# Other durations in the planning clock while the S5 tables are made

## The chip, the cores and the metric

The kernel runs on one core of a Trainium2 chip. The metric is the time of one execution on the device in microseconds (us). The core has five engines with a queue of instructions each: TensorE (PE in the rows) multiplies matrices into banks of PSUM, VectorE (DVE) and ScalarE (ACT) work element by element, GpSimd (POOL) does so more slowly, and SyncE (SP) issues the transfers (DMA).

## The reference

One step of a decoder layer on a prompt of 2048 rows of 1024 numbers and on 8 samples of 4 rows, all in float32. Cut to its core:

```python
h = rms_norm(x, attn_norm)
u, q, k, v, g, z = jnp.split(h @ w_in, [c1, c2, c3, c4, c5], axis=-1)
# S5: 32 groups of 16 channels with 64 complex states each
dt = jnp.exp(log_step)[:, None]
mag = jnp.exp(A_re * dt)
lam_r, lam_i = mag * jnp.cos(A_im * dt), mag * jnp.sin(A_im * dt)
# s_t = lam * s_{t-1} + Bb u_t;  y = Re(C s) + D u; then GELU, GLU, norm
y5, s5_re, s5_im = s5_mixer(u, ...)
# GLA: chunks of 64 rows, b = cumsum(log sigmoid(z w + b) / 16)
qe, ke = qc * jnp.exp(b), kc * jnp.exp(-b)
o = mask(qe ke^T) vc + qe S
x = x + jnp.concatenate([y5, o], axis=-1) @ w_o
a, b = jnp.split(rms_norm(x, ffn_norm) @ w_up, 2, axis=-1)
x = x + (silu(causal_dwconv3(a)) * b) @ w_down
```

The outputs are the normalised rows and the new states of S5, GLA and the convolution.

## The kernel before, in words

The prompt is cut into four windows (w0 to w3) of 512 rows; w1 carries the 32 sample rows too, 544 in all. For each window the rows of x are normalised and transposed, TensorE makes the gate inputs z, the channels u, the gates' sums, q and k, then v tile by tile with the attention (GLA), then g, and then the projection by W_o's part for the attention. After the windows come the S5 scan, GLU and W_o's other half beside the first part of the feed-forward (blocks of `up`), and then a last stage of block products for the rest of it. Every float32 matrix is split into a rounded half (`hi`, float32r) and the rest (`lo`), and a product takes three matmuls. A weight block is loaded by SP, its `hi` made on ScalarE or GpSimd and its `lo` on GpSimd or VectorE, as `make` (line 666) decides from the clocks of the engines.

The program order is fixed: the instructions stand on each engine in the order in which the Python code emits them. The code of the windows emits the matmuls of its projections, and between groups of them calls `tick` (line 395). That lets generators emit pieces of other work: the tables of S5 (`gen_tables`, line 902, run by `gen_first`, line 1585), the transposed rows of the next window (`gen_hT`, line 839, which starts when five tile slots are free), the attention's tiles, S5 and GLU. How much of it comes where is decided by a planning clock (`Clock`, line 176). Each emitted instruction adds to it an assumed duration on its engine, behind the assumed ends of its inputs (`Clock.op`, line 237; the durations stand in `Engine`, line 280). A piece is emitted when its inputs have arrived on that clock, and work of low priority only while VectorE and ScalarE are at most 9 us ahead of TensorE on it. So a number in the clock changes no instruction, but its place in the queues.

The tables of S5 are made once, on VectorE, ScalarE and TensorE: from A and the step a chain of small operations on 16 partitions (exponential, sine, reciprocal, coefficients), powers by repeated products, transposes of 16 columns, copies and scalings of the powers (tiles of 64 x 144 and 64 x 288), and eight blocks, each with 16 products, two additions, transposes on TensorE and stores of Cd, Bd and Td to DRAM. GLA needs of VectorE the running sums (scans), and the product of q and k with exponentials (made on ScalarE); these products drain the banks `mm` of PSUM. Transposes and small products use the banks `bg`. Tiles are `t_L`, `t_H` (large and half) and `pair_L` (halves). Since each instruction goes through one helper, all rows show line L290 (L292 in the changed program).

Of the kernel before, what the change touches and what calls it, by code (L numbers as in the profile page):

```python
# [175 lines left out]
class Clock:  # L176
# [5 lines left out]
    def __init__(self):  # L182
        self.eng = {"PE": 0.0, "V": 0.0, "A": 0.0, "G": 0.0, "SP": 0.0}
        self.dma = 0.0
        self.ready = {}
        self.last = {}
        self.seen = {}
        self.stored = {}
        self.banks = {}
        Clock.parts = {}  # L190
# [89 lines left out]
class Engine:  # L280
# [5 lines left out]
    def __getattr__(self, name):  # L286
        fn = getattr(self.e, name)

        def call(*args, **kw):
            r = fn(*args, **kw)  # L290
            aps = [x for x in args if _names(x)]
            aps += [v for n, v in kw.items() if _names(v) and n != "accum_out"]  # L292
            out, ins = aps[:1], aps[1:]
            n = 1
            for d in out[0].shape[1:]:
                n *= d
            psum = any(str(getattr(x, "space", "")).endswith("PSUM") for x in aps)
            names = [q for x in ins for q in _names(x)]
            outs = [q for x in out + [kw[z] for z in ("accum_out",) if z in kw] for q in _names(x)]
            if name == "dma_start":  # L300
                m = 4
                for d in ins[0].shape:
                    m *= d
                t_ = self.c.dma_op(self.k, m, *([] if self.c.span(x)[0] else q for x, q in ((out[0], outs), (ins[0], names))), out[0], ins[0])
                return r
            if self.k == "PE":
                if kw.get("is_t") or name == "transpose":
                    cost = 0.005 + 1e-3 * n
                elif str(ins[0].dtype).endswith("float32r"):
                    cost = max(n / 2400 + 0.004, 0.11)  # L310
                else:
                    cost = max(4 * n / 2400, 0.11)
            elif self.k == "A":
                cost = 0.05 + 0.87e-3 * n
                table = TABLES.get(args[2] if len(args) > 2 else kw.get("func"))
                if table not in (None, self.table):
                    self.table = table
                    cost += 1.3
            elif self.k == "G":
                cost = 0.3 + 0.165 * n if kw.get("op") == ALU.pow else 0.12 + (2.15e-3 if name == "tensor_tensor" else 0.88e-3) * n  # L320
            else:
                fast = name in ("tensor_copy", "tensor_scalar") and not psum
                cost = 0.07 + (0.52e-3 if fast else 1.04e-3) * n
            t_ = self.c.op(self.k, cost, outs, names)
            return r

        return call
# [98 lines left out]
def kernel(ctx: ExitStack, tc: tile.TileContext, ins, outs):  # L426
# [17 lines left out]
    clock = Clock()  # L444
# [3 lines left out]
    PE, V, A, G, SP = (Engine(clock, k, e) for k, e in (  # L448
        ("PE", nc.tensor), ("V", nc.vector), ("A", nc.scalar), ("G", nc.gpsimd), ("SP", nc.sync)))
# [1134 lines left out]

    def gen_first():
        yield from gen_tables()
        flags.add("tables")

    s5 = [[bg.add(4 + hf, gen_s5(hf, q)) for q in range(4)] for hf in range(2)]
# [393 lines left out]
    for w in range(NWIN):  # L1983
        bg.most = MOST[w]
        smp = w == SW
        n = XC if smp else WT
        pieces = ((0, 272), (272, 544)) if smp else ((0, 512),)
        bg.drain(hT[w, 0], hT[w, 1], *([hT["s"]] if smp else []))
        if w == 0:
            setup_masks()  # L1990
            bg.add(2, gen_first())
# [624 lines left out]
    for kind, c, j in items:  # L2616
# [13 lines left out]
        for p in (1, 2, 3, 6, 4, 7, 5):  # L2630
# [23 lines left out]
            elif end:  # L2654
# [5 lines left out]
                while late and late[0] in stage and (p not in (1, 2) or kind == "down"):  # L2660
                    q = late.pop(0)
# [49 lines left out]
```

## Time and profile before

| | before |
|---|---|
| median of three runs | 2420.09 us (2413.03 to 2422.62) |
| profiled execution | 2419.89 us, span 2418.2 us |
| mean granted clock of TensorE | 0.971 of 2.4 GHz |
| TensorE busy | 2282.5 us, 94% |
| VectorE busy | 1545.2 us, 64% |
| ScalarE busy | 896.8 us, 37% |
| GpSimd busy | 539.0 us, 22% |

The span runs from the first to the last instruction; the rest of the profiled execution lies around it. Busy shares are averages over stages with different limits. Where TensorE is 94% busy, its timeline shows the few places where it waits, and behind each wait stands what ended it. A granted clock below 1.00 in a stretch means that TensorE ran part of it at 1.2 GHz.

### The profile page before, as it was taken

What the parts mean: (1) busy time and instruction counts of PE and PEld (TensorE: products, weight loads), DVE (VectorE), ACT (ScalarE), POOL (GpSimd) and SP (SyncE); (2) the same over time, 40 slices, a digit from 0 to 9 for tenths busy, and PEclk for the clock granted to TensorE, in tenths of its full rate; (3) what the DMA queues carried; (4) which work ended last, traced back from release to release, by engine and by line L of the source; (5) the groups of instructions that cost most, each with busy time, mean ns of one, the idle gap of its engine ahead of it and who ended that gap; (6) DMA issues with size and microseconds to landing.
All of it is one profiled execution on the core that took longest, in us unless ns stands there. A gap on an engine that the chain in (4) does not pass through costs nothing.

```text
span 2418.2 us, 32048 instructions
## 1 busy us (share of the span) xinstructions
PE 2282.5 (94%) x11809; PEld 1933.0 (80%) x11809; DVE 1545.2 (64%) x2743; ACT 896.8 (37%) x1634; POOL 539.0 (22%) x645
## 2 busy tenths in 40 slices
PE   7798999999999899999998998999999998999998
PEld 5577877777787689999998997887888776777776
DVE  6777547866633467654436655666666778686887
ACT  3243144434422453243233113344443435343444
POOL 5245425546432435631010010000000000000011
PEclk9899999999999999999999999999999999999999
DMA  6124546426653723344544752222222478676754
GB/s 170 62 94 132 149 121 196 115 83 200 174 168 112 252 93 106 114 143 121 168 166 142 249 177 62 68 81 87 79 79 79 147 232 267 226 247 215 242 184 151
DMA packets 357021, 359.72 MB, mean 149 GB/s; under 512 B 56546, under 2 KB 274842, under 8 KB 356864
## 3 DMA queue, kind: packets, MB, share of 16 engines
q1 hardware_dynamic: 356512, 357.53, 47.0%
q8 instruction: 93, 1.52, 0.3%
q14 instruction: 64, 0.52, 0.1%
q10 hardware_dynamic: 352, 0.15, 0.0%
HBM read 250.99 MB, written 106.62 MB: 148 GB/s over the span
## 4 chain that ended last, share of the span: by engine, by line
PE 61%; DVE 16%; ACT 6%; issue 4%; POOL 3%; DMA 1%; SPq 0%; ACTq 0%; DVEq 0%; POOLq 0%
PE all L290 42%; DVE t_L L290 13%; PE mm L290 11%; PE bg L290 8%; ACT t_L L290 5%; DVE t_H L290 2%; DVE pair_L L290 2%; POOL t_H L290 1%; POOL t_L L290 1%; POOL pair_L L290 1%; DMA t_L<-in_w_o_dram 0%; ACT t_H L290 0%; ACT pair_L L290 0%; DMA t_L<-Wd 0%; SPq L290 0%
## 5 line engine op out<-in xcount | busy, mean ns | idle before, releaser
L290 PE MATMUL all<-t_L,t_L 128*128 128x512 f32 (+4 forms) x7358 | 1472.2, 361 | 51.0 <-DVE t_L L290 20.0
L290 PEld LDWEIGHTS all<-t_L,t_L 128*128 128x128 f32 (+2 forms) x7358 | 1280.0, 189 | 236.4 <-DVE t_L L290 36.0
L290 DVE TENSOR_TENSOR t_L<-t_L,t_L 128x1024 fp32r<-128x1024 f32 (+9 forms) x636 | 553.0, 896 | 175.5 <-ACT t_L L290 116.3
L290 ACT ACTIVATE t_L<-t_L 128x1024 fp32r<-128x1024 f32 (+8 forms) x450 | 361.9, 825 | 440.8 <-DVE t_L L290 360.3
L290 PE MATMUL mm<-t_L,t_L 128*128 128x512 f32 (+2 forms) x2160 | 491.5, 384 | 15.4 <-DVE t_L L290 12.3
L290 PEld LDWEIGHTS mm<-t_L,t_L 128*128 128x128 f32 (+1 forms) x2160 | 382.6, 191 | 100.5 <-issue 17.5
L290 POOL TENSOR_SCALAR rr<-ss 128x1 f32<-128x1 f32 (+1 forms) x51 | 19.7, 386 | 1044.7 <-ACT pair_L L290 955.2
L290 DVE TENSOR_TENSOR t_L<-t_L,all 128x512 f32<-128x512 f32 (+2 forms) x268 | 172.4, 643 | 101.8 <-PE all L290 37.9
L290 POOL TENSOR_SCALAR t_L<-t_L 128x1024 fp32r<-128x1024 f32 (+1 forms) x91 | 117.4, 1298 | 320.5 <-PE all L290 146.7
L290 POOL TENSOR_TENSOR t_L<-t_L,t_L 128x1024 fp32r<-128x1024 f32 x49 | 136.3, 2784 | 51.8 <-ACT t_L L290 39.6
L290 ACT ACTIVATE t_L<-all 128x512 f32<-128x512 f32 (+2 forms) x134 | 71.6, 539 | 191.0 <-PE all L290 186.1
L290 DVE TENSOR_TENSOR t_L<-t_L,pair_L 128x512 f32<-128x512 f32 (+2 forms) x138 | 93.4, 679 | 56.4 <-ACT pair_L L290 51.4
L290 ACT ACTIVATE pair_L<-all 128x512 f32<-128x512 f32 (+1 forms) x104 | 61.6, 593 | 154.1 <-PE all L290 134.1
L290 PE MATMUL bg<-t_L,t_L 128*128 128x256 f32 (+7 forms) x628 | 111.2, 344 | 2.3 <-DVE t_H L290 2.3
L290 DVE SCALAR_TENSOR_TENSOR t_L<-all,cw,t_L 128x351 f32<-128x351 f32 (+1 forms) x132 | 74.7, 566 | 48.0 <-ACT t_L L290 47.2
L290 PEld LDWEIGHTS bg<-t_L,t_L 128*128 128x128 f32 (+4 forms) x628 | 85.1, 183 | 24.6 <-issue 10.8
L290 ACT ACTIVATE t_L<-all,cw 128x352 f32<-128x352 f32 x66 | 42.4, 642 | 147.1 <-PE all L290 130.2
L290 ACT ACTIVATE t_L<-bg 128x512 fp32r<-128x512 f32 (+7 forms) x121 | 53.5, 461 | 103.8 <-PE bg L290 99.3
L290 DVE SCALAR_TENSOR_TENSOR t_L<-t_L,cw,t_L 128x1024 f32<-128x1024 f32 x44 | 56.5, 1285 | 24.6 <-ACT t_L L290 23.8
L290 ACT ACTIVATE junk<-bg 128x128 bf16<-128x128 f32 (+1 forms) x68 | 18.8, 276 | 120.5 <-PE bg L290 118.9
L290 ACT ACT_TABLE_LOAD x41 | 52.6, 1283 | 23.0 <-DVE t_L L290 14.7
L290 DVE TENSOR_TENSOR t_L<-pair_L,t_L 128x144 f32<-128x144 f32 (+5 forms) x107 | 54.6, 538 | 8.2 <-ACT pair_L L290 5.8
(180 smaller groups left out, 1643.4 us busy)
## 6 DMA issues: line engine op xcount, KB each, us to landing
t_L<-in_w_up_dram SPq DMA_DIRECT2D x88, 512.0 KB, 4.9
t_L<-x2d SPq DMA_DIRECT2D x80, 512.0 KB, 5.9
t_L<-in_w_in_dram SPq DMA_DIRECT2D x64, 512.0 KB, 5.5
x2d<-t_L SPq DMA_DIRECT2D x48, 512.0 KB, 3.1
gT<-t_L SPq DMA_DIRECT2D x44, 512.0 KB, 2.7
t_L<-gT SPq DMA_DIRECT2D x48, 384.0 KB, 4.8
t_L<-in_w_down_dram SPq DMA_DIRECT2D x34, 512.0 KB, 4.9
t_L<-in_w_o_dram SPq DMA_DIRECT2D x24, 512.0 KB, 5.5
```

Source lines behind the costliest of these rows:

```text
L290: r = fn(*args, **kw)
```

## The change

While the tables are made, the clock takes longer durations: 0.0135 instead of 0.004 us over the columns for a float32r matmul, 0.155 instead of 0.05 for ScalarE, 0.14 instead of 0.07 for VectorE. A VectorE instruction with two inputs or more, none in PSUM, that would start within the last two-input operation of GpSimd is taken to wait for its end. When `gen_tables` has ended, the former figures hold again.

```diff
@@ Clock.__init__
+        self.fine = True
+        self.sums = (0.0, 0.0)
@@ Engine, the durations
-                    cost = max(n / 2400 + 0.004, 0.11)
+                    cost = max(n / 2400 + (0.0135 if self.c.fine else 0.004), 0.11)
...
-                cost = 0.05 + 0.87e-3 * n
+                cost = (0.155 if self.c.fine else 0.05) + 0.87e-3 * n
...
-                cost = 0.07 + (0.52e-3 if fast else 1.04e-3) * n
+                cost = (0.14 if self.c.fine else 0.07) + (0.52e-3 if fast else 1.04e-3) * n
+                if self.c.fine and not psum and len(aps) > 2:
+
+                    g0, g1 = self.c.sums
+                    t = max([self.c.eng["V"]] + [self.c.arrive("V", q) for q in names])
+                    if g0 <= t < g1:
+                        cost += g1 - t
             t_ = self.c.op(self.k, cost, outs, names)
+            if self.k == "G" and name == "tensor_tensor":
+                self.c.sums = t_
@@ gen_first
         yield from gen_tables()
+        clock.fine = False
         flags.add("tables")
```

What it moves. First VectorE in window 0, from the reciprocal of the tables to the first products of q and k; `mm_457` and `mm_489` are the banks with q, `mm_521` and `mm_553` those with k, `t_L_319` is a table on 16 partitions. In the program before:

```order
63 L290 RECIPROCAL t_L_319<-t_L_319 16x128
64 L290 TENSOR_SCALAR t_L_319<-t_L_432 16x128
65 L290 TENSOR_TENSOR t_H_298<-t_L_319,t_H_298 16x128
66 L290 TENSOR_TENSOR t_L_319<-t_L_433,t_H_299 16x128
67 L290 TENSOR_TENSOR t_H_298<-t_H_298,t_L_319 16x128 x2
68 L290 TENSOR_TENSOR t_H_299<-t_L_433,t_H_298 16x128
69 L290 TENSOR_TENSOR t_L_319<-t_L_319,t_H_299 16x128
70 L290 TENSOR_TENSOR t_H_299<-t_H_299,t_L_319 16x128 x2
71 L290 SCALAR_TENSOR_TENSOR t_L_453<-mm_457,t_L_453 128x512
72 L290 SCALAR_TENSOR_TENSOR t_L_453<-mm_489,t_L_453 128x512
73 L290 TENSOR_TENSOR t_L_454<-mm_521,t_L_454 128x512
74 L290 TENSOR_TENSOR t_L_454<-mm_553,t_L_454 128x512
```

In the changed program, from the subtraction of the running sum (`t_L_392`) to the products of k; the banks with q are `mm_409` and `mm_441`, those with k `mm_473` and `mm_522`:

```order
46 L292 TENSOR_TENSOR t_L_392<-t_L_392,pair_L_400 128x512 x2
47 L292 SCALAR_TENSOR_TENSOR t_L_405<-mm_409,t_L_405 128x512
48 L292 SCALAR_TENSOR_TENSOR t_L_405<-mm_441,t_L_405 128x512
49 L292 TENSOR_TENSOR t_L_319<-t_H_298,sm_321 16x128
50 L292 TENSOR_TENSOR t_L_319<-t_H_299,sm_321 16x128
51 L292 TENSOR_SCALAR t_L_319<-t_L_319 16x128 x3
52 L292 SCALAR_TENSOR_TENSOR t_L_319<-t_L_319 16x128 x2
53 L292 TENSOR_SCALAR pair_L_320<-t_L_319 16x128
54 L292 TENSOR_SCALAR t_L_319<-t_L_319 16x128
55 L292 SCALAR_TENSOR_TENSOR t_L_319<-t_L_319 16x128 x7
56 L292 SCALAR_TENSOR_TENSOR t_L_319<-t_L_319,pair_L_320 16x128
57 L292 TENSOR_TENSOR t_L_406<-mm_473,t_L_406 128x512
```

The 17 operations of the table's exponential, which stood ahead of the scans, now stand between the products of q and of k; the sine, the reciprocal and the coefficients come behind all four products.

Second, VectorE in the projection W_o of window 0. Before, the end of the first block of tables stands there, from its last four products to the drains `mm` of W_o:

```order
222 L290 TENSOR_TENSOR t_L_1441<-pair_L_1242,t_L_1091 128x144
223 L290 TENSOR_TENSOR t_L_1442<-pair_L_1242,t_L_1091 128x144
224 L290 TENSOR_TENSOR pair_L_1235<-pair_L_1152,t_L_1068 128x128
225 L290 TENSOR_TENSOR pair_L_1152<-pair_L_1235,t_L_1068 128x128
226 L290 TENSOR_TENSOR t_L_1441<-t_L_1441,t_L_1442 128x576
227 L290 TENSOR_TENSOR pair_L_1235<-pair_L_1235,pair_L_1152 128x512
228 L290 TENSOR_TENSOR t_H_1391<-t_H_1391,mm_1463 128x512
```

In the changed program the copies and scalings of the powers stand between the four drains of W_o's second half there, and `bg_1488` holds the transposed sample rows:

```order
199 L292 COPY t_L_1419<-pair_L_1255 64x144 x8
200 L292 TENSOR_TENSOR t_H_1401<-t_H_1401,mm_1431 128x512
201 L292 SCALAR_TENSOR_TENSOR t_L_1379<-t_L_1379,rr_1383,gain 32x1024
202 L292 TENSOR_TENSOR pair_L_1255<-pair_L_1255,mm_1449 128x512
203 L292 COPY t_L_1463<-t_L_1419 64x288
204 L292 TENSOR_SCALAR t_L_1463<-t_L_1419 64x288 x3
205 L292 TENSOR_SCALAR t_L_1419<-t_L_1419 64x32
206 L292 COPY t_L_1419<-t_L_1419 64x32
207 L292 TENSOR_SCALAR t_L_1419<-t_L_1419 64x32
208 L292 COPY t_L_1419<-t_L_1419 64x32
209 L292 TENSOR_SCALAR t_L_1419<-t_L_1419 128x32
210 L292 TENSOR_TENSOR t_H_1447<-t_H_1447,mm_1474 128x512
```

The first block went from here to the first matmuls of window 1, behind its gate sums; the copies came here from the attention of window 0.

Third, TensorE at the end of window 1. Before, from the transposed x rows of window 2 (`t_L_3034` and the like) over those of the sample's output (`t_H_2973`) and a product with it:

```order
1448 L290 MATMUL bg_3274<-ident,t_L_3034 128x128
1449 L290 MATMUL bg_3274<-ident,t_L_3036 128x128
1450 L290 MATMUL bg_3281<-ident,t_H_2973 128x32 x4
1451 L290 MATMUL mm_3297<-t_L_2845,t_L_3286 64x512
1452 L290 MATMUL mm_3297<-t_L_2846,t_L_3286 32x512
```

In the changed program at this place, from a group of W_o (`mm_3048`) over the sample's state (`bg_3086` and the like), the transposes and the product of the last block of tables (`bg_3110`, `bg_3117`), to the sample's output (`pair_L_2402`):

```order
1424 L292 MATMUL mm_3048<-t_L_2806,t_L_2970 128x512
1425 L292 MATMUL bg_3086<-pair_L_2291,t_L_2401 64x128 x8
1426 L292 MATMUL bg_3096<-pair_L_2291,t_L_2401 64x128 x8
1427 L292 MATMUL bg_3110<-ident,pair_L_2696 128x128 x4
1428 L292 MATMUL bg_3117<-t_L_3062,t_H_1508 16x128 x4
1429 L292 MATMUL bg_3125<-pair_L_2291,t_L_2401 64x128 x8
1430 L292 MATMUL bg_3135<-pair_L_2291,t_L_2401 64x128 x8
1431 L292 MATMUL bg_3172<-ident,pair_L_2402 128x32 x4
1432 L292 MATMUL mm_3189<-t_L_2692,t_L_3177 64x512
```

Before, the last block lay far ahead of this place, and 16 of the 32 transposes of x rows ahead of the sample's output, 16 behind the product with it. Now the last block lies here, and all 32 transposes follow behind the last group of W_o and the first groups of S5.

## Rows read from the trace of the kernel before

**Rows 1.** Busy time (and count) of each engine by stretch, then TensorE's granted clock.

```profile
140.00:180.00 40.00, 35.51 (x165) 29.02 (x166) 37.40 (x52) 23.66 (x44) 24.99 (x20) 0.91 0.34 108
190.00:203.00 13.00, 4.78 (x22) 3.64 (x21) 13.00 (x19) 0.00 (x0) 9.63 (x5) 0.79 0.24 74
213.00:218.00 5.00, 5.00 (x42) 4.43 (x39) 4.89 (x19) 0.77 (x2) 0.00 (x0) 1.00 0.42 101
220.00:340.00 120.00, 120.00 (x738) 97.73 (x738) 65.56 (x185) 40.22 (x84) 44.44 (x24) 1.00 0.44 118
```

**Rows 2.** Timeline of TensorE, first wait: start, duration, operation, [wait before, releaser].

```profile
71.84 12.34 PE L290 MATMUL mm<-t_L,t_L 128*128 128x512 f32 x40 [10.71 <-DVE t_L L290]
```

**Rows 3.** Timeline of VectorE around the first wait.

```profile
52.92 2.19 DVE L290 COPY decay<-t_L 128x8 f32<-128x8 f32 x1
...
58.65 4.26 DVE L290 TENSOR_TENSOR t_L<-t_L,pair_L 128x512 f32<-128x512 f32 x2
...
63.33 0.91 DVE L290 SCALAR_TENSOR_TENSOR t_L<-t_L 16x128 f32<-16x128 f32 x3
...
71.03 1.27 DVE L290 SCALAR_TENSOR_TENSOR t_L<-mm,t_L 128x512 f32<-128x512 f32 x2
```

**Rows 4.** Timelines of GpSimd and ScalarE around the first wait.

```profile
51.91 3.18 POOL L290 TENSOR_TENSOR t_L<-t_L,t_L 128x1024 fp32r<-128x1024 f32 x1
...
59.69 2.68 POOL L290 TENSOR_TENSOR t_L<-t_L,t_L 128x1024 fp32r<-128x1024 f32 x1
70.98 7.07 POOL L290 TENSOR_TENSOR t_L<-t_L,t_L 128x1024 fp32r<-128x1024 f32 x3 [8.61 <-ACT t_L L290]
...
67.96 4.85 ACT L290 ACTIVATE t_L<-t_L 128x1024 f32<-128x1024 f32 x5
```

**Rows 5.** Timelines of VectorE and TensorE at the second wait.

```profile
146.11 5.56 DVE L290 COPY t_L<-t_H 64x144 f32<-64x144 f32 x8
...
152.02 3.10 DVE L290 TENSOR_SCALAR t_L<-t_L 64x288 f32<-64x288 f32 x4
...
157.68 2.79 PE L290 MATMUL bg<-ident,pair_L 128*128 128x128 f32 x12 [3.59 <-DVE pair_L L290]
```

**Rows 6.** Timelines of VectorE and TensorE at the third wait.

```profile
189.88 1.30 DVE L290 TENSOR_TENSOR t_L<-pair_L,t_L 128x144 f32<-128x144 f32 x2
...
202.19 0.67 DVE L290 TENSOR_TENSOR pair_L<-pair_L,pair_L 128x512 f32<-128x512 f32 x1
...
203.01 1.09 PE L290 MATMUL bg<-ident,pair_L 128*128 128x128 f32 x4 [8.23 <-DVE pair_L L290]
203.74 4.86 PE L290 MATMUL mm<-t_L,t_L 128*128 128x512 f32 x12
```

**Rows 7.** Timeline of VectorE, first and last row of the second block.

```profile
213.17 0.52 DVE L290 TENSOR_TENSOR t_L<-pair_L,t_L 128x144 f32<-128x144 f32 x2
...
217.20 0.69 DVE L290 TENSOR_TENSOR t_H<-t_H,t_H 128x512 f32<-128x512 f32 x1
```

**Rows 8.** Timelines of SP, VectorE and TensorE before window 2; DMA: KB, median us to landing.

```profile
333.99 5.02 SPq L290 DMA_DIRECT2D Td<-t_L  x8
...
350.21 2.02 SPq L290 DMA_DIRECT2D t_L<-in_x_prompt_dram  x4
...
t_L<-in_x_prompt_dram SPq DMA_DIRECT2D x4, 512.0 KB, 5.9
...
370.35 5.73 DVE L290 SCALAR_TENSOR_TENSOR t_L<-t_L,rr,gain 128x1024 f32<-128x1024 f32 x4
...
375.79 1.09 PE L290 MATMUL bg<-pair_L,t_L 32*64 32x128 f32 x16
...
384.58 0.43 PE L290 MATMUL bg<-ident,t_H 32*128 32x32 f32 x4 [1.82 <-DVE t_L L290]
386.57 3.67 PE L290 MATMUL mm<-t_L,t_L 128*64 128x512 f32 x8 [1.56 <-DVE t_L L290]
...
392.70 11.15 PE L290 MATMUL mm<-t_L,t_L 128*128 128x512 f32 x48
```

## The prediction

> **What bounds the kernel now.** I read the busy times first: TensorE works 94% of the span, so the change can win only where TensorE waits or runs at its lower clock. The busy times by stretch come next: from 220 to 340 us TensorE has no gap and the full clock, from 140 to 180 us the granted clock is 0.91, a mean over its two levels of 1.2 and 2.4 GHz [rows 1]. TensorE's own timeline then shows where it waits while the S5 tables are made, in window 0: 10.71 us before 71.84, 3.59 us before 157.68 and 8.23 us before 203.01, each released by VectorE [rows 2, 5, 6]. Last I read the timelines of VectorE and GpSimd over the same stretches, to see what VectorE did in these waits. The change moves instructions from early in the program to about the start of window 2; in the last stage TensorE's list is the same in both programs. So I add up four places.
>
> **Place 1, the drains of q and k in window 0.** TensorE has finished its groups at 61.13 (71.84 - 10.71) and needs a bank of PSUM that VectorE must drain. VectorE ends the subtraction of the running sum at 58.65 + 4.26 = 62.91, then makes 25 small table operations, with ScalarE between, and drains the first two banks only from 71.03 [rows 2, 3]. In the changed list these two drains stand right behind the subtraction. They need the exponential on ScalarE, about 0.97 us (4.85 for 5) [rows 4]: 62.91 + 0.97 + 0.64 (half of 1.27 for two drains) = 64.5, so TensorE would go on 7.3 us earlier. But only for twelve matmuls, as the third bank is drained behind 17 table operations that stood earlier before. At 0.30 us each (three in 0.91) [rows 3] these are 5.2 us, from 65.2 to 70.4, and the drain ends at 71.0. Twelve matmuls take 2.8 us at full clock (48 in 11.15) [rows 8] and, by that, 5.6 at half; with some of both TensorE waits again from about 68 to 71. The waits sum up to 3.4 + 3 = 6.4 instead of 10.7: 4.3 gained. The other bound: GpSimd now makes the rounded half of three more weight blocks here, where it stood idle from 62.4 (59.69 + 2.68) to 70.98 [rows 4]. A copy of 128x8 at 52.92 took 2.19 us, more than seven times the 0.30 of a larger operation, and ended at 55.11 with GpSimd's subtraction, 51.91 + 3.18 = 55.09 [rows 3, 4]. With three such holds of 2.1 each the gain is gone and 2 us more are lost. I take 2 gained, since a block's multiplication leaves VectorE free for part of the time; range from 4.3 gained to 2 lost.
>
> The diff lets only operations with two inputs wait for GpSimd, and that copy has one. The Trainium skill (SBUF — State Buffer, Who interferes with whom) says that copies and one-input scalar operations can take the port shared with GpSimd too, and that the second to issue is blocked for the whole instruction; the trace agrees for this copy. By that rule all 17 operations are exposed and place 1 loses the 2 us; by the diff's own rule only some are, and it gains up to 4.3.
>
> **Place 2, copies and scalings of the powers.** Before, eight copies (5.56 us) and four scalings (3.10) stand between the outputs of window 0's attention and their transposes: TensorE waits 3.59 us, and the lower clock around it costs 0.09 x 40 = 3.6 us [rows 1, 5]. In the changed list they stand in the projection W_o, where four banks lie between TensorE and VectorE. These 7.2 us go. What is late next: four groups of twelve matmuls give 11.2 us of cover; VectorE has there four drains (0.67 each, as the addition at 202.19) [rows 6], the copies, the scalings, one normalisation of 1.43 (5.73 for 4) [rows 8] and six small operations, about 1 us by the 0.30 of the small ones in place 1 and less for fewer columns: 13.8. So the last drain and the sample rows behind it come 2.6 us late, and behind them ScalarE and GpSimd still make the operands of window 1's first matmul, some 1 to 2 us; with part of that at half clock I take 4, from a range of 0 to 7.
>
> **Place 3, the first block of tables.** The 18 operations of a block took from 189.88 to 202.86 with GpSimd at work, and from 213.17 to 217.89 while it was idle (first and last rows shown) [rows 1, 6, 7]. TensorE waited 8.23, and the next twelve matmuls took 4.86 instead of 2.79, with four transposes 1.09: about 2.4 us of clock [rows 6, 8]. These 10.6 us go. In the changed list 84 matmuls of 272 columns stand between the last input of VectorE and this block's transposes, some 84 x 0.13 = 11 us (0.232 for 512 columns, so 0.12 to 0.14 here). Against that stand 4.7 us alone and 13.0 beside GpSimd, with two clears and a product ahead. I take 0 for a new wait and keep 5 as its other end.
>
> **Place 4, from the last table to window 2.** This one costs. Tables now end later in TensorE's list, and the last block stands on VectorE right behind a drain of W_o, while TensorE has only two small sample groups (1.09 us each) [rows 8] to do before its transposes: 0.67 + 4.7 - 2.2 = 3.2 us of wait. The sample's state follows on VectorE, three multiplications (1.43 by the nearest row), four additions and a subtraction (0.67), 7.6 us against 3.2 us on TensorE: 4.4 us before the sample's transposes, where the trace has 1.82, and behind them again about 1.56, as before [rows 8]. That is 9.2 against 3.4: 5.8 lost.
> Then the x rows of window 2, which SP issues behind the last eight table stores. Counted from the end of the block: state additions 7.6, stores 5.02, issues 2.02, landing 5.9, square 0.97, normalisation 1.43, in all 22.9; if the four rows share the way in and land twice as late, 28.8 [rows 4, 8]. TensorE gets there after 7.6 + 1.6 + 3.7 (eight matmuls at half clock) + 11.15 (W_o) + about 4 (sample and S5, from the same row) = 28 [rows 8]. So the 32 transposes, all behind W_o now, just find their rows, and each us of delay on SP or VectorE beyond that is one on TensorE. I take 1.5. Place 4 together: 7.3 lost, from 4 to 25.
>
> **Sum.** -2 - 7.2 + 4 - 10.6 + 7.3 = -8.5. The rest of the stages before the last keep their work, shifted against each other; I give that 0, with 5 either way. The profiled execution took 2419.89 us (span 2418.2), within 0.2 of the median of the runs, 2420.09: 2419.89 - 8.5 is about 2411.
>
> **Rivals.**
> *All of it is won.* Place 1 gains 4.3, window 1 starts without a wait and place 4 costs 5: -4.3 - 7.2 - 10.6 + 5 = -17.1, 2403. For it: the later blocks of tables in window 1 cost TensorE nothing before, from 220 to 340 us [rows 1]. Against it: place 2's 13.8 us on VectorE under 11.2 on TensorE.
> *GpSimd holds VectorE back at the new places.* The 17 operations at place 1 (2 lost), the block at the start of window 1 (5 lost), the copies and the wait behind them (7 lost): 2 + 5 + 7 - 7.2 - 10.6 + 7.3 = +3.5, 2423. For it: the slow rows of rows 3 and 6 lie beside GpSimd. It is also what the skill's rule on the port gives where copies and scalings are held as well. Against it: from 213 to 218, where the trace has its second block, GpSimd did nothing [rows 1].
> *Slower: window 2 waits for its x rows and weights.* The rows stand on SP behind stores that wait for VectorE's last addition, the weights behind the rows and the loads of S5. If the rows land 5.9 us later, the next weights another 5.9, with 2.7 for their subtraction (59.69), and 6 us of clock follow, under twice place 2's 3.6: -8.5 + 20.5 = +12, 2432, and up to 2440. It decides from the point where the rows land after W_o and S5 end. For it: all 32 transposes come in one piece, where half stood ahead of W_o. Against it: 22.9 against 28.
>
> **How the numbers follow.** The forecast has 0.36 (2406 to 2417), all won 0.29, held back 0.20, slower 0.15. A measurement of this kernel tells about 0.5%, 12 us, from no change: faster is under 2408, slower over 2432. All won is faster but for a tenth of it, and the forecast by a quarter: 0.35. Slower takes two thirds of the last case and a little of the third: 0.13. The rest, 0.52, is the same. The range runs from 2396 to 2435, which leaves out the ends of the first and the last case, about 2 in 10 with what I have not thought of.
>
> **What would show it.** Place 1: VectorE's first drain of q at about 64.5 and a second wait of some 3 us before the third bank. Place 2: no idle before the transposes of window 0's outputs, a wait of 3 to 4 us before window 1's first matmuls. Place 3: a block in 5 to 8 us without a wait on TensorE. Place 4: waits of about 3, 4 and 1.6 us, and transposes of x rows with under 2 us of idle. A stall of over 10 us before window 2's first matmul, or a first drain after 68, would prove the forecast wrong.

## The result, and the profile after

The changed kernel takes 2441.24 us (median of 4 runs, 2440.91 to 2442.94), the kernel before on the same chip 2421.36: a ratio of 1.0089, 95% interval 1.0068 to 1.0110. It is slower by about 20 us, where 8.5 less than before, about 2411, were forecast. The profiled execution has a span of 2439.7 us against 2418.2, so 21.5 us are to be found.

The table cuts the spans at TensorE's first matmul of each window (`mm<-t_L,wz`), at the first matmul of 352 columns, with which the stage behind window 3 begins, and at the start of the last product of that stage. Idle is the sum of the gaps between TensorE's rows; half is TensorE's busy time in the pieces in which the profile has the granted clock at 0.5, and costs half of itself. All in us.

| stage | length before | idle | half | length after | idle | half | difference |
|---|---|---|---|---|---|---|---|
| window 0 | 192.2 | 27.0 | 30.3 | 174.0 | 16.1 | 14.6 | -18.2 |
| window 1 | 196.8 | 4.4 | 5.5 | 226.5 | 24.7 | 23.6 | +29.7 |
| window 2 | 195.2 | 12.2 | 18.4 | 207.4 | 19.6 | 23.2 | +12.2 |
| window 3 | 242.7 | 16.9 | 9.1 | 236.9 | 12.5 | 7.2 | -5.8 |
| next stage | 640.1 | 19.9 | 17.1 | 640.9 | 20.6 | 19.9 | +0.8 |
| last stage | 931.1 | 42.2 | 16.2 | 933.9 | 42.2 | 22.6 | +2.8 |

Length less idle less half of half is the work at full clock, and it is the same in each stage within 2.5 us (window 1: 189.6 and 190.0). So no work was added or moved between stages: TensorE waits elsewhere, and runs at the lower clock where it waited. Window 0 gained about what was forecast (15.8 in the sum), though not where; windows 1 and 2 lost 41.9.

Busy times of three stretches, first of before, then of after (stretch, then length, busy time and count of TensorE, weight loads, VectorE, ScalarE, GpSimd; granted clock, DMA share, GB/s):

```profile
100.00:140.00 40.00, 37.82 (x207) 28.25 (x205) 12.20 (x45) 7.61 (x32) 6.02 (x7) 0.83 0.15 53
360.00:440.00 80.00, 76.62 (x426) 60.90 (x425) 62.39 (x89) 40.89 (x132) 46.87 (x59) 0.96 0.64 181
```
```profile
100.00:140.00 40.00, 40.00 (x212) 30.51 (x212) 19.98 (x45) 14.23 (x40) 9.63 (x10) 1.00 0.21 67
140.00:180.00 40.00, 35.77 (x192) 28.75 (x191) 38.30 (x49) 16.18 (x31) 31.10 (x21) 0.91 0.41 122
360.00:440.00 80.00, 59.45 (x289) 43.68 (x287) 36.76 (x67) 27.27 (x81) 35.97 (x45) 0.77 0.56 166
```

From 360 to 440 us every engine does less than before, so none is the bound there; they wait for each other. From 100 to 140 us the wait of 2.2 and the half clock of this stretch are gone: 2.2 + 0.17 x 40 = 9.0 us, at a place that the prediction does not have. And at place 2, from 140 to 180 us, nothing is won: busy time 35.77 for 35.51 and the same clock of 0.91 [rows 1, 5].

**Place 1** [rows 2 to 4]. After, timelines of TensorE, VectorE and GpSimd (start, duration, operation, count, [wait before, releaser]):

```profile
64.28 5.46 PE L292 MATMUL mm<-t_L,t_L 128*128 128x512 f32 x12 [3.71 <-DVE t_L L292]
76.55 5.63 PE L292 MATMUL mm<-t_L,t_L 128*128 128x512 f32 x16 [6.82 <-DVE t_L L292]
...
63.44 1.29 DVE L292 SCALAR_TENSOR_TENSOR t_L<-mm,t_L 128x512 f32<-128x512 f32 x2 [1.12 <-ACT t_L L292]
64.64 2.22 DVE L292 TENSOR_TENSOR t_L<-t_H,sm 16x128 f32<-16x128 f32 x2
66.79 3.53 DVE L292 TENSOR_SCALAR t_L<-t_L 16x128 f32<-16x128 f32 x3
70.35 2.77 DVE L292 SCALAR_TENSOR_TENSOR t_L<-t_L 16x128 f32<-16x128 f32 x2
...
66.81 2.42 POOL L292 TENSOR_TENSOR t_L<-t_L,t_L 128x1024 fp32r<-128x1024 f32 x1
69.20 1.04 POOL L292 TENSOR_SCALAR t_L<-t_L 128x1024 fp32r<-128x1024 f32 x1
70.33 2.34 POOL L292 TENSOR_TENSOR t_L<-t_L,t_L 128x1024 fp32r<-128x1024 f32 x1
```

The first drain comes at 63.44 and TensorE goes on at 64.28, as forecast (64.5). The second wait is 6.82 instead of 3: three of VectorE's rows among the 17 small operations take 1.6 to 2.6 us longer than 0.30 for each operation, beside GpSimd. Together 10.53 against 10.71.

**Place 3** [rows 6, 7]. After, VectorE, GpSimd and TensorE at the first block:

```profile
199.67 7.45 DVE L292 COPY t_H<-t_L 64x128 f32<-64x128 f32 x4
207.15 3.42 DVE L292 TENSOR_TENSOR t_L<-t_L,t_L 128x1024 fp32r<-128x1024 f32 x1
...
214.88 0.44 DVE L292 TENSOR_TENSOR t_L<-pair_L,t_L 128x144 f32<-128x144 f32 x2
...
218.85 0.67 DVE L292 TENSOR_TENSOR pair_L<-pair_L,pair_L 128x512 f32<-128x512 f32 x1
...
199.42 3.01 POOL L292 TENSOR_TENSOR t_L<-t_L,t_L 128x1024 fp32r<-128x1024 f32 x1
202.40 1.07 POOL L292 TENSOR_SCALAR t_L<-t_L 128x1024 fp32r<-128x1024 f32 x1
203.55 2.39 POOL L292 TENSOR_TENSOR t_L<-t_L,t_L 128x1024 fp32r<-128x1024 f32 x1
205.91 1.09 POOL L292 TENSOR_SCALAR t_L<-t_L 128x1024 fp32r<-128x1024 f32 x1
207.09 2.40 POOL L292 TENSOR_TENSOR t_L<-t_L,t_L 128x1024 fp32r<-128x1024 f32 x1
...
201.88 10.82 PE L292 MATMUL mm<-t_L,t_L 128*128 128x272 f32 x84
219.58 1.11 PE L292 MATMUL bg<-ident,pair_L 128*128 128x128 f32 x4 [6.88 <-DVE pair_L L292]
```

The block itself takes 4.7 us (214.88 to 219.52) and the cover 10.82, both as worked out. But VectorE comes to it late: the four copies ahead, which the prediction did not count, take 7.45 us beside GpSimd. One by one they take 2.88, 1.02, 2.48 and 1.03: each ends within 0.13 us of one of GpSimd's instructions, the one-input scalings as well as the sums. The wait of 8.23 is one of 6.88 in the next window.

**Place 4** [rows 8]. After, SP's queue, VectorE and TensorE from the last block to window 2:

```profile
380.17 5.87 SPq L292 DMA_DIRECT2D Td<-t_L  x8
386.14 1.95 SPq L292 DMA_DIRECT2D t_L<-in_x_prompt_dram  x4
388.14 0.75 SPq L292 DMA_DIRECT2D t_L<-Ud  x1
...
398.20 1.88 SPq L292 DMA_DIRECT2D t_L<-in_w_in_dram  x2
400.19 1.82 SPq L292 DMA_DIRECT2D pair_L<-in_x_prompt_dram  x1
...
407.26 1.37 DVE L292 TENSOR_TENSOR pair_L<-pair_L,mm 128x512 f32<-128x512 f32 x2 [17.24 <-DMA pair_L<-in_x_prompt_dram]
408.56 1.86 DVE L292 SCALAR_TENSOR_TENSOR t_L<-t_L,rr,gain 128x1024 f32<-128x1024 f32 x1
...
424.16 0.67 DVE L292 TENSOR_TENSOR t_H<-t_L,t_L 128x128 f32<-128x128 f32 x2 [4.37 <-POOL t_L L292]
...
371.61 1.09 PE L292 MATMUL bg<-ident,pair_L 128*128 128x128 f32 x4 [3.61 <-DVE pair_L L292]
...
380.75 0.60 PE L292 MATMUL bg<-ident,pair_L 32*128 32x32 f32 x4 [1.82 <-DVE pair_L L292]
...
410.56 0.45 PE L292 MATMUL bg<-ident,t_L 128*128 128x128 f32 x1 [6.43 <-DVE t_L L292]
412.31 3.46 PE L292 MATMUL bg<-ident,t_L 128*128 128x128 f32 x15 [1.30 <-DVE t_L L292]
417.32 3.68 PE L292 MATMUL bg<-ident,t_L 128*128 128x128 f32 x16 [1.55 <-DVE t_L L292]
...
426.23 2.34 PE L292 MATMUL mm<-t_L,wz 128*32 128x512 f32 x5 [3.79 <-DVE t_L L292]
```

Window 2's rows are asked for at 386.14 instead of 350.21. They land in time: ScalarE has squared the last of them by 395.98. Their scaling is late. It stands on VectorE behind the drains of W_o, and these wait 17.24 us for the other rows, those that W_o's result is added to. SP issues these only at 400.19, behind S5's first loads and window 2's weights. TensorE waits 6.43, 1.30 and 1.55 for the rows. The last wait, 3.79, is for the rows' last three `lo` halves, which VectorE makes from 425.50: ahead of them in its list stands a step of S5 (424.16), for which it waits 4.37 until GpSimd has made the step before. The clock is at half from 407.83 to 421.48 and from 424.89 to 431.72.

Window 2's longest wait behind this grew as well; the first row here is from before, the second from after:

```profile
496.77 0.49 PE L290 MATMUL bg<-pair_L,t_H 128*128 128x128 f32 x2 [3.23 <-DVE t_H L290]
```
```profile
513.87 0.77 PE L292 MATMUL bg<-pair_L,t_H 128*128 128x128 f32 x2 [8.38 <-DVE t_H L292]
```

### The profile page after: what moved, and what is told of

It reads as the page before. It is cut to its first block, busy times and chain, and to the rows that moved or that the text cites. A ratio compares the mean times of both kernels' runs of the same rounds, so it can differ in the third digit from the quotient of the medians.

```text
span 2439.7 us, 32035 instructions
## 1 busy us (share of the span) xinstructions
PE 2291.1 (94%) x11809; PEld 1938.4 (79%) x11809; DVE 1542.5 (63%) x2736; ACT 892.2 (37%) x1636; POOL 536.3 (22%) x647
## 4 chain that ended last, share of the span: by engine, by line
PE 45%; DVE 14%; ACT 6%; issue 4%; POOL 2%; DMA 2%; SPq 1%; DVEq 0%; POOLq 0%; ACTq 0%
PE all L292 39%; DVE t_L L292 12%; ACT t_L L292 6%; PE bg L292 3%; PE mm L292 3%; DVE t_H L292 2%; POOL t_H L292 1%; SPq L292 1%; DMA t_H<-in_x_prompt_dram 1%; POOL t_L L292 0%; ACT pair_L L292 0%; DMA t_L<-ydT 0%; DMA pair_L<-Wd 0%; DMA t_L<-in_w_in_dram 0%; ACT t_H L292 0%
## 5 line engine op out<-in xcount | busy, mean ns | idle before, releaser
L292 PEld LDWEIGHTS all<-t_L,t_L 128*128 128x128 f32 (+2 forms) x7358 | 1281.9, 189 | 242.7 <-DVE t_L L292 34.7
L292 DVE TENSOR_TENSOR t_L<-t_L,t_L 128x1024 fp32r<-128x1024 f32 (+7 forms) x639 | 554.9, 894 | 193.1 <-ACT t_L L292 142.2
L292 PE MATMUL mm<-t_L,t_L 128*128 128x512 f32 (+2 forms) x2160 | 493.6, 385 | 16.2 <-DVE t_L L292 15.3
L292 POOL TENSOR_SCALAR t_L<-t_L 128x1024 fp32r<-128x1024 f32 (+1 forms) x96 | 123.1, 1286 | 352.9 <-PE all L292 132.6
L292 DVE TENSOR_TENSOR t_L<-t_L,pair_L 128x512 f32<-128x512 f32 (+3 forms) x139 | 94.3, 681 | 75.6 <-ACT pair_L L292 54.0
L292 POOL TENSOR_TENSOR t_L<-t_L,t_L 128x1024 fp32r<-128x1024 f32 x46 | 125.7, 2732 | 22.2 <-ACT t_L L292 18.4
L292 PE MATMUL bg<-ident,t_L 128*128 128x128 f32 (+2 forms) x256 | 45.2, 313 | 24.5 <-DVE t_L L292 24.5
L292 POOL TENSOR_TENSOR t_H<-t_H,t_L 128x128 f32<-128x128 f32 (+5 forms) x90 | 46.8, 541 | 75.1 <-DVE t_H L292 34.3
```

## The experiments

All times in one table; ratio to before on the same chip, stage lengths from the profiled execution. In the texts on record "after" is the changed kernel and "before" the other.

| kernel | us | ratio [95%] | window 0 | 1 and 2 | 3 | next | last |
|---|---|---|---|---|---|---|---|
| before | 2421.36 | 1 | 192 | 392 | 243 | 640 | 931 |
| after | 2441.24 | 1.0089 [1.0068, 1.0110] | 174 | 434 | 237 | 641 | 934 |
| e1 | 2464.64 | 1.0174 [1.0155, 1.0194] | 173 | 425 | 263 | 652 | 932 |
| e2 | 2439.05 | 1.0070 [1.0055, 1.0085] | 173 | 432 | 240 | 641 | 934 |
| e3 | 2451.42 | 1.0129 [1.0111, 1.0147] | 189 | 385 | 283 | 643 | 930 |
| e4 | 2464.55 | 1.0181 [1.0164, 1.0198] | 174 | 423 | 266 | 642 | 930 |
| e5 | 2430.68 | 1.0039 [1.0027, 1.0051] | 174 | 432 | 234 | 640 | 930 |
| e6 | 2446.34 | 1.0102 [1.0075, 1.0129] | 195 | 418 | 242 | 640 | 929 |
| e7 | 2437.01 | 1.0062 [1.0041, 1.0083] | 190 | 435 | 225 | 639 | 933 |
| e8 | 2435.15 | 1.0052 [1.0033, 1.0071] | 193 | 451 | 213 | 626 | 930 |
| e9 | 2440.28 | 1.0084 [1.0066, 1.0102] | 195 | 416 | 237 | 640 | 930 |
| e10 | 2458.66 | 1.0166 [1.0136, 1.0196] | 173 | 427 | 261 | 643 | 930 |
| e11 | 2459.80 | 1.0162 [1.0145, 1.0179] | 191 | 403 | 260 | 651 | 929 |
| e12 | 2434.13 | 1.0064 [1.0041, 1.0087] | 174 | 430 | 242 | 641 | 930 |
| e13 | 2429.03 | 1.0039 [1.0022, 1.0056] | 174 | 417 | 242 | 641 | 934 |
| e14 (after) | 2436.26 | 1.0071 [1.0051, 1.0091] | 174 | 432 | 239 | 640 | 930 |
| e15 | 2420.47 | 1.0007 [0.9991, 1.0024] | 193 | 391 | 244 | 640 | 930 |
| e16 | 2427.90 | 1.0042 [1.0024, 1.0060] | 174 | 419 | 242 | 640 | 931 |

**Parts of the change alone (e1, e6, e7, e8, e11).** e1 turns the new figures off when window 1 begins; e8 has them only from there on:

```diff
+        if w == 1:
+            clock.fine = False
```


> The changed kernel, but with the former figures from the start of window 1. Theory A (the loss is made where the last block of tables meets the end of window 1: SP has the loads of S5 ahead of the residual rows of W_o, VectorE waits for those in its list, and the x rows of window 2 behind them): window 0 is as in the changed kernel, first matmul of window 1 near 195 us, the tables end earlier in TensorE's list, the 17 us wait of VectorE for residual rows goes, 2405 to 2417 us. Theory B (VectorE is too full in window 1 with all eight blocks beside GpSimd, the boundary only inherits it): little better than the changed kernel, 2430 to 2441 us.

> The former figures in window 0, the new ones from the start of window 1 to the end of the tables. Window 0 is then as in before (window 1's first matmul at 209 to 213). The tables end at 216 us of TensorE's work, nearly as in before (219). Theory C: windows 1 and 2 take 390 to 400 us as in before, time 2415 to 2425. Theory D (any new order of window 1 by the new figures loses at its end): windows 1 and 2 take 415 or more, time 2440 to 2465.

e6 keeps only the matmul's new duration, e7 only the rule for GpSimd sums, e11 all but VectorE's new duration (e11's edit; e6 and e7 put back the other former figures in the same way):

```diff
-                cost = (0.14 if self.c.fine else 0.07) + (0.52e-3 if fast else 1.04e-3) * n
+                cost = 0.07 + (0.52e-3 if fast else 1.04e-3) * n
```


> Only the new duration of a matmul is kept (while the tables are made); ScalarE's and VectorE's durations and the rule for GpSimd sums are the former ones. In this order the tables end a fifth earlier by TensorE's work than in after (183 us of work in place of 233). Theory C (how late the tables end decides the loss: their last blocks, S5's first loads and window 2's rows and weights meet at the end of window 1 when it is late, and not when it is early): windows 1 and 2 together take 385 to 400 us, and the time is 2400 to 2420. Theory D (the loss is one of the order as a whole, whichever table time): 2425 to 2450, with windows 1 and 2 at 410 or more.

> Only the rule that an operation of VectorE with two inputs in SBUF ends with the GpSimd sum beside it is kept (while the tables are made); all durations are the former ones. The tables end at 190 us of TensorE's work (after 233, before 219). Theory C: windows 1 and 2 take 385 to 400 us, time 2400 to 2420; whether the 18 us gained in window 0 come from this rule is read from window 1's first matmul, 194 if they do and 212 if not. Theory D: 2425 to 2450.

> The changed kernel with the former fixed duration of VectorE's operations (0.07 us in place of 0.14); the new durations of the matmul and of ScalarE and the rule for GpSimd sums stay. The tables then end at 215 us of TensorE's work (after 234, before 221), and window 2's rows are asked for 36 us of work before its first matmul (after 14, before 30). Theory E: windows 1 and 2 take 390 to 405 us, and if the new rule keeps window 0 short (window 1 at 194 to 200) the time is 2400 to 2418. Theory F: windows 1 and 2 take 410 or more, time 2425 to 2445.

No part alone is faster than before, and window 0 is short (173, 174) only where all the new figures stand in it. e6 and e7 end the tables early (last table store at 312 and 317 us, after 385) and still need 418 and 435 us for windows 1 and 2: it isn't the end of the tables as such, and theory C falls. In e8 window 1 begins at 213.4 as in before, and 1 and 2 take 451, partly since they do 22 us more of TensorE's work than before, mostly products of GLU, which window 3 then lacks; in e7 it is 11 us. In e11 windows 1 and 2 come nearest to before (403), but it loses 18 in window 3 and 11 behind it, with a wait of 10.08 before the first transposes there. e1, e3, e4 and e10 show a wait of the same size (9.99 to 10.22), where before has 5.65. It is none of after's loss, and its cause stays open; no theory foresaw the loss in window 3, and the times of e1, e3, e10 and e11 lie above both of their theories' ranges. e8's time, 2435.15, lies between its two ranges, though windows 1 and 2 are as in theory D.

**The last rows on another queue (e2), S5 later (e4), one block later (e3).** e2 issues the W_o rows of window 1 from ScalarE's queue once the tables are made, all else in the same order:

```diff
+            clock.alt = A.e if w == SW and "tables" in flags else None
```


> The changed kernel with the same order on every engine, but the residual rows of W_o in window 1, from the end of the tables on, are issued on ScalarE's queue instead of SP's. Theory A: VectorE's 17.2 us wait for these rows shrinks to under 5, the waits of TensorE before window 2 (6.4, 1.3, 1.6, 3.8 us) fall to under 5 together, 2425 to 2432 us. Theory B: the rows were not what held it, at most 3 us less, 2438 to 2442 us.

VectorE's wait of 17.24 is gone, the rows are transposed 6 us earlier, and TensorE waits 7.99 a little later. TensorE, VectorE, ScalarE and GpSimd in e2:

```profile
424.12 2.34 PE L293 MATMUL mm<-t_L,wz 128*32 128x512 f32 x5 [7.99 <-DVE t_L L293]
...
411.10 3.22 DVE L293 TENSOR_TENSOR t_L<-bg,t_L 128x512 fp32r<-128x512 f32 x5 [7.95 <-ACT t_L L293]
422.05 0.67 DVE L293 TENSOR_TENSOR t_H<-t_L,t_L 128x128 f32<-128x128 f32 x2 [7.74 <-POOL t_L L293]
...
410.46 2.07 ACT L293 ACTIVATE t_L<-bg 128x512 fp32r<-128x512 f32 x4
...
421.50 0.52 POOL L293 TENSOR_TENSOR t_L<-t_L,t_H 128x128 f32<-128x128 f32 x1
```

ScalarE copies S5's first products until 410.46 before it turns to the rows' halves, which holds VectorE's first five `lo` halves. The wait of 7.99 is for the last three, and these stand behind the same step of S5 as in after: VectorE waits 7.74 for GpSimd, which makes S5's steps until 422.02. So the next two lists were as full as SP's, and window 2 goes on only 2.1 us earlier than in after (424.12 for 426.23).

e4 starts S5 only in window 2; e3 is before with its last table block held until W_o's fourth step:

```diff
-        need = [("u", 2 * hf, q), ("u", 2 * hf + 1, q), "tables"] + ([("s5", 0, q), ("st", 0, "c")] if hf else [("us", q), "gs"])
+        need = [("u", 2 * hf, q), ("u", 2 * hf + 1, q), "tables", ("win", 2)] + ([("s5", 0, q), ("st", 0, "c")] if hf else [("us", q), "gs"])
```
```diff
+            while q == 7 and "hold" not in flags:
+                yield "idle"
```


> The changed kernel, but S5 may begin only when window 2 has begun, so that its loads do not stand on SP ahead of the residual rows of W_o. Theory A: the wait before window 2 falls to under 5 us, 2425 to 2434 us, unless S5 coming later costs it again in window 2. Theory B: 2438 us or more.

> The kernel before with its former figures, but the last block of tables is held back until W_o of window 1 has emitted its fourth step. Window 0 and most of window 1 are as before. Theory A: a wait of TensorE of 10 us or more appears before window 2, as in the changed kernel, 2432 to 2446 us. Theory B: within 4 us of before, 2417 to 2425 us.

e4 takes 11 less in windows 1 and 2 and 29 more in window 3. But 8 of the 11 are work of TensorE that has left these windows, so hardly anything is won. e3 takes 7 less than before in windows 1 and 2, at 14 us less work there, so 7 are lost, and 40 more in window 3, of which 17 are work. Late rows (they are loaded at 373 there) cost little in e3, in which S5 has not begun: TensorE waits 4.80 for them.

**The copies (e5, e13, e14, e15, e16).** e5 is after in its own order, with the four copies of place 3 made by ScalarE:

```diff
+        clock.cp = A.e
         for r_ in range(2):
             for q in range(2):
                 V.tensor_copy(ss5[r_ * 64 : r_ * 64 + 64, q::2], s0v[q * 64 : q * 64 + 64, r_])
+        clock.cp = None
```


> The order of after, word for word; only the four copies t_H<-t_L 64x128 of the first table block, which took 7.45 us on VectorE at 199.67 beside the GpSimd sums of window 1, are made by ScalarE at the same place in the program. Theory A (these copies, held beside the GpSimd sums, are what TensorE's wait of 6.88 at 219.58 rests on, and the wait costs the time): VectorE comes to the block some 7 us earlier, the wait falls under 1.5 us, window 1's first matmul stays at 194 and window 2's comes at 411 to 414, and the time is 2431 to 2435. Theory B (what is gained early in window 1 is given back at its end, where TensorE waits for rows and tables): the wait falls as well, window 2 begins at 418 to 421, and the time is 2438 to 2442.

ScalarE and TensorE in e5:

```profile
195.58 0.87 ACT L292 ACTIVATE t_H<-t_L 64x128 f32<-64x128 f32 x2
...
214.02 0.66 PE L292 MATMUL bg<-ident,pair_L 128*128 128x128 f32 x4 [1.48 <-DVE pair_L L292]
...
223.85 2.43 PE L292 MATMUL mm<-t_L,t_L 128*128 128x272 f32 x11 [3.14 <-ACT pair_L L292]
```

Two copies take 0.87 us there. The wait of 6.88 becomes 1.48, but 3.14 more come right behind it, and window 2 begins only 1.4 us earlier: theory B early on. The time is 10.6 under after's first result. e14, after once more on e5's chip, takes 2436.26, between the two values expected, with 10.6 us at half clock in the last stage instead of 22.6.

> The changed kernel itself once more, on the chip of e12 and e13. 2438 to 2443 if its time is as steady from chip to chip as that of before; under 2435 if e5's 2430.68 was the chip or the granted clock.

So 5.6 of the 10.6 are e5's. But the profiles do not show them at the copies: windows 0 to 2 together are as long in e5 as in e14 within 0.5 us, and 4.8 of the difference stand in window 3, at the same idle time within 1 us and with 3.3 us at half clock instead of 11.4. So what the copies cost by their wait is not shown to be 5 us. e13 against e12 gives 5.1 (on one chip), with intervals of the ratios that overlap.

> As e12, word for word, with the four copies of the first block on ScalarE as in e5. If the copies cost time by the wait behind them: 5 to 10 us under e12. If e5's gain was the granted clock of the later stages: within 3 us of e12, or to either side by what the clock's half-speed stretches differ.

e15 does the same in before, with the copies and scalings of the powers too (place 2), and e16 in e12:

> The kernel before, in its order, with the one-input operations of two table steps made by ScalarE at the same places of the program: the copies and scalings of the powers (5.56 us and the scalings behind them on VectorE, before 157.68) and the copies into the first block. If place 2 was sized rightly (the wait of 3.59 us goes, and the lower clock around it): window 1's first matmul at 205 to 208 in place of 212.4, and the time is 2413 to 2417 if the rest stays. If what is gained in window 0 is given back before window 3, as in after: window 3 begins at 602 to 606 as in before, time 2418 to 2424. Slower, if ScalarE, which goes through its list in order, comes late with the halves of the weights behind the copies: 2424 to 2430.

> e12 with both sets of copies and the scalings on ScalarE. The copies into the first block were worth 5 us (e13 against e12). The copies of the powers stand in the projection W_o of window 0 in this order, where no wait of TensorE rests on them, so they should be worth 0 to 2: 2426 to 2430. If they were what the wait of 1.46 before window 1 rests on, window 1 begins 1 to 2 us earlier.

e15 is before's time within the noise. The wait of 3.59 [rows 5] is gone from its place and others stand there, in all 5.22. TensorE in e15:

```profile
154.04 3.05 PE L293 MATMUL mm<-t_L,t_L 128*128 128x512 f32 x12 [1.94 <-ACT t_H L293]
158.27 0.63 PE L293 MATMUL bg<-ident,pair_L 128*128 128x128 f32 x4 [1.18 <-DVE pair_L L293]
159.94 0.63 PE L293 MATMUL bg<-ident,pair_L 128*128 128x128 f32 x4 [1.05 <-DVE pair_L L293]
161.62 1.09 PE L293 MATMUL bg<-ident,pair_L 128*128 128x128 f32 x4 [1.05 <-DVE pair_L L293]
```

**The rows of window 2 (e9, e10, e12).** e9 is before, with these four loads held back to W_o's third step; the tables and S5's first loads stay:

```diff
+        while w == SW + 1 and "hold" not in flags:
+            yield "idle"
         if w:
             yield from room(5)
```


> The kernel before, with one edit: the rows of window 2 (four loads t_L<-x_prompt, at 350 us in before, when the tables end) are asked for only after the second W_o step of window 1, at about 385 us as in after. The tables and S5's first loads stay where they are. Theory E (the lead of window 2's rows decides the loss at the end of window 1: rows asked for after S5's loads come behind them, and VectorE's scalings of the rows behind the W_o drains): window 2's first matmul comes 10 to 20 us later than in before, at 419 to 430, and the time is 2432 to 2445. Theory F (the rows are only one of several waits there, and when one goes or comes another moves): window 2 begins at 409 to 416, time 2418 to 2430.

The loads go out at 391.24 instead of 350.21, window 2 begins at 434.0 instead of 409.1, and the time is 2440.28, that of after (2.4 of the 24.9 stand in window 0 already). So holding these rows back, with what the planner then puts in their place, is enough to lose all of it. How, these rows of TensorE in e9 tell:

```profile
400.58 5.85 PE L290 MATMUL mm<-t_L,t_L 128*64 128x512 f32 x15 [11.06 <-DVE t_L L290]
...
410.87 11.48 PE L290 MATMUL mm<-t_L,t_L 128*128 128x512 f32 x41 [4.44 <-POOL t_L L290]
...
429.19 1.12 PE L290 MATMUL bg<-ident,t_L 128*128 128x128 f32 x4 [5.09 <-DVE t_L L290]
```

Only the last of the three is for the rows; the first is the sample's W_o step, whose input stands on VectorE behind S5 operations that took the place of the rows' scalings (one of them waits 4.00 for GpSimd). The sum is as in theory E, the waits are not.

e10 lets after's rows go when two tiles are free instead of five; e12 puts the tables first in window 1, so that they end, and the rows are loaded, earlier:

```diff
-            yield from room(5)
+            yield from room(2 if w == SW + 1 else 5)
```
```diff
+        if w == SW:
+            for e in bg.gens:
+                if e[0] == 2 and e[3].__name__ == "gen_first":
+                    e[:2] = [0, -1]
+            bg.gens.sort(key=lambda e: e[:2])
```


> The changed kernel, with one edit: the rows of window 2 wait for two free tiles in place of five, so the first two loads come 25 us of TensorE's work before after's, and the last two a little before; the tables still end late (237 us of work, 234 in after). Theory E: the wait of 6.43 us before the transposes of window 2's rows goes, window 2's first matmul comes at 405 to 412, and the time is 2420 to 2432. Theory F: window 2 begins at 415 to 425 and the time is 2435 to 2450.

> The changed kernel with one rule more: from the start of window 1 the tables come before all other work that is merged in. Window 0 is word for word that of after up to the end of the table preparation; the tables end at 214 us of TensorE's work (after 234, before 221), and window 2's rows are asked for 38 us of work before its first matmul (after 14, before 30). Theory E (the tables' late end, and with it the rows' late loads, is what costs after its gain): window 1 at 194, windows 1 and 2 take 388 to 400 us, and the time is 2400 to 2418. Theory F (the end of window 1 loses in every order but that of before): windows 1 and 2 take 410 or more, time 2425 to 2445.

e10's first rows load at 324, but the last table block then waits on VectorE for tiles that are still being stored (1.17 and 4.25), and TensorE for the block 8.70. VectorE's wait for the W_o rows is there as in after, 16.70, and behind it TensorE waits 8.17 before window 2: with the rows of window 2 transposed early it begins at 421.06, as in after (420.65). In e12 all rows go out at 345.50, no transpose of them waits, and window 2 takes 192.6, less than in before. Window 1 takes 237.4. TensorE in e12:

```profile
217.92 1.12 PE L292 MATMUL bg<-ident,pair_L 128*128 128x128 f32 x4 [7.10 <-DVE t_L L292]
...
228.83 1.12 PE L292 MATMUL bg<-ident,t_H 128*128 128x128 f32 x4 [5.56 <-DVE t_H L292]
...
402.25 3.67 PE L292 MATMUL mm<-t_L,t_L 128*64 128x512 f32 x8 [4.16 <-DVE t_L L292]
...
413.16 0.50 PE L292 MATMUL mm<-t_L,t_L 128*128 128x512 f32 x1 [3.33 <-ACT t_L L292]
```

Two waits of table blocks at its start, and at its end the sample's step again and the halves of W_o's weights, behind S5's copies on ScalarE. Theory F, then, for after: each repair tried moves the wait to the next user of the same lists. The best of these, e5, e13 and e16 (1.0039, 1.0039 and 1.0042, after 1.0071 and 1.0089), stay above before; no kernel here beats it.

## Why the prediction was wrong

By its own terms, in the profiled executions:

- *Place 1*, "2 gained": 0.2 in the waits (10.53 against 10.71). The forecast of the first drain and of a second wait was right, the second wait's size not: 6.82 for 3. The reason given for taking 2, that a multiplication on GpSimd leaves VectorE free, is not in the rows: the last of VectorE's operations at 66.79 ends at 70.32, GpSimd's scaling beside it at 70.24. The trace agrees with what the Trainium skill states of the port shared with GpSimd (SBUF — State Buffer, Who interferes with whom): one-input operations are held too, three scalings of 16x128 for 3.53 us beside a GpSimd sum of 2.42 and a scaling of 1.04, where three operations of that size took 0.91 [rows 3].
- *Place 2*, -7.2 + 4: 1.1 lost. The wait of 3.59 is gone, but shorter ones and another piece at half clock stand in the same 40 us (0.3 more busy time, 0.91 as before), and window 1's first matmul waits 1.35 instead of 4. e15 shows the same for the copies alone, with the wait gone and the granted clock still 0.91: the clock's 3.6 was no gain that hangs on this wait. It was also too large, since in part of the half clock TensorE waited; its 5.7 us of work there cost 2.9.
- *Place 3*, 10.6 gained, "I take 0 for a new wait and keep 5 as its other end": the new wait is 6.88, with 2.0 of clock (3.9 us of TensorE's work at half behind it, until 223.51), so 1.7 were gained. I counted the block and its cover, and not what VectorE has in its list ahead of the block: four one-input copies beside GpSimd.
- Not priced: 9.0 gained from 100 to 140 us, where a wait of 2.2 before `bg<-t_H,t_H` went, and the half clock with it. I took the three longest waits of window 0 and left out this fourth one, whose stretch cost 9.0 with its clock.
- *Place 4*, "Place 4 together: 7.3 lost, from 4 to 25": this is the step that failed. Windows 1 and 2 lost 41.9, less 8.9 for the first block: 33.0. The last block and the sample were sized about rightly, 5.8 forecast and 7.0 lost: the waits are shorter together than forecast (3.61, 1.82 and 0.69 for 3.2, 4.4 and 1.6), but 12.5 us of work behind them ran at half clock (from 370.28 to 387.35), where before has 5.5. The x rows failed: "I take 1.5", and they cost 19.9, 13.1 in waits (6.43 + 1.30 + 1.55 + 3.79) and 6.8 for 13.6 us of work at half clock around them. The other 6.1 are window 2's, the largest piece the wait of 8.38 where before had 3.23, which the forecast has at nothing. The sign named for a wrong forecast, over 10 us of stall before window 2's first matmul, came in pieces: 9.3 before it and 3.79 behind its first five matmuls. The count of 22.9 to 28.8 against 28 followed one chain, from the table stores to these rows, and no clock behind a wait. It left out that VectorE takes the rows only after the W_o drains, that these wait for rows that SP issues behind S5's loads, and that S5's first steps stand on VectorE ahead of the rows' last halves.
- *The other stages*, "0, with 5 either way": -2.2, and 0.5 is left over in window 0. Right.

-0.2 + 1.1 - 1.7 - 9.0 + 33.0 - 1.7 = 21.5.

The outcome is the rival "Slower: window 2 waits for its x rows and weights" (2432, up to 2440), at its place and 1 us past its end. I gave it 0.15, since its one chain came out at 22.9 against 28. Its number is nearer than its mechanism: it lets the rows land late, and they landed in time; late were their scaling, behind the W_o rows, and their last halves, behind S5. What the runs show: holding these rows back, with what the planner then puts in their place, is enough to cost before 19 us (e9). What they do not show is one cause in after: with the rows early again (e12) or the other rows on another queue (e2) 12 and 17 us of loss stay, and with S5 later (e4) it goes to window 3. Where the 33 us stand is read from the trace, as above; how much of them each of the tables' last blocks, the rows, the sample's step and S5's first work causes stays open, since none could be moved without the planner moving the others.

## What to carry to other kernels

Where several streams of work meet on engines that take their lists in order, a wait that a new order removes is not a gain until the next operation in that list is known to be ready: e2, e5, e12 and e15 each removed the wait they aimed at, and TensorE waited for another. Price the meeting place by everything that stands in the list ahead of the late operation, and its inputs, not by one chain. And an order in which a stretch has almost no wait (before's window 1, 4.4 us) is the thing to protect: all other orders of windows 1 and 2 tried here but three (e3, e11, e15) lost 24 us or more there.

## What was not expected of the hardware

- Four copies of 64x128 in SBUF took VectorE 7.45 us beside GpSimd, each until one of GpSimd's instructions ended, two sums (3.01 and 2.39) and the scalings behind them (1.07 and 1.09). ScalarE made two of the copies in 0.87. The kernel's new rule counts only operations with two inputs, on VectorE and on GpSimd.
- The same program differs between two measurements mainly by the granted clock: the changed kernel took 2441.24 and 2436.26 in two measurements (before, beside them: 2421.36 and 2421.93), its last stage 933.9 with 22.6 us at half clock and 930.3 with 10.6, at the same idle time within 2 us. A difference of 5 us between two orders of this kernel says little without the stage lengths.
